# Lower halves and sums of squares of the first mixers on VectorE, and the spatial gate's scale and shift behind its mix

## The chip, the cores and the metric

The kernel runs on one core of a Trainium2 chip. The metric is the device time in microseconds (us) of one execution. The kernel before was timed three times: 3413.01, 3419.14 and 3424.70 us, so the median is 3419.14 us. Its profile is one further execution, with a span of 3426.9 us.

## What is computed

Two transformer blocks run over 512 tokens of 1024 features. Only the first block's mixers are touched by the change, and a part of the second block's memory that is prepared among them:

```
a = rmsnorm(h, g_mix);  z = a @ w_in                       # 1024 -> 2304 features
ya = conformer_conv(z[:768])      # val*sigmoid(gate), 31 taps in time, group layernorm, silu
yb = short_gated_conv(z[768:1536])                         # 3 taps, two gates
yc = spatial_gating(z[1536:])                              # below
h  = h + concatenate([ya, yb, yc]) @ w_out                 # then the experts, block 2, ...

def spatial_gating(zc, ln_g, ln_b, w_s, b_s):
    u, v = split(zc)
    v = group_layernorm(v, ln_g, ln_b, 6 heads of 64)      # (v - m) * rstd * g + b
    ws = w_s masked by chunks of 64 positions              # [head, i, j], i and j in 0..127
    mixed = einsum("hij,bnjhc->bnihc", ws, v) + b_s        # over each block of 128 tokens
    return u * mixed
```

The second block needs `rmsnorm(mem) @ w_mem_kv` for 256 memory rows. It depends on nothing else, so the kernel computes it here.

## The kernel before, in words

All products of this part keep float32 accuracy by a split: a raw tile is rounded to a high half on ScalarE (`hi`, line 163), and the low half `raw - hi` is computed by a second engine (line 164). TensorE then makes three products for each pair (lines 180 to 182): high by high, high by low and low by high. `load_split` (line 165) does this for a chunk of weights. It has three raw tiles (`wir`), two high tiles (`wih`) and two low tiles (`wil`), and `eng` names the engine of the low half.

`front` is the part that the change touches. It runs in this order:

1. The norm of the 512 tokens, split into `xh` and `xl`, eight feature tiles of 128x512.
2. Six products `ftile` of 128 features each (24 matmuls of 512 columns) for the conformer's gate and value, which give `y` (line 326).
3. The value half of the spatial gate, token-major, in four chunks of 128x768 weights, evacuated to `vn` (line 340), then its group norm: 24 statistics (lines 343 and 344), a reciprocal root by Newton's method (`rsqrt`, lines 193 to 198), 24 small subtract-and-multiply operations on VectorE (line 352), and scale and shift on GpSimd (lines 353 and 354).
4. Six products for the short convolution (lines 360 to 373), then the mix of `vn` with `wsT` (line 380) and three products `ftile(12 + hp)`.
5. `memprep`: the memory, eight tiles of 128x256, split into `memh` and `meml`, with sums of squares (`sqa`, lines 130 and 132).
6. The long convolution (`cv`, lines 394 and 397): three times 31 operations of 128x512 on VectorE.
7. The conformer's tail (lines 403 to 424): three chains that go back and forth between TensorE, VectorE and ScalarE.
8. `memkv`: eight chunks for keys (24 matmuls of 256 columns) and eight for values (12 matmuls of 512 columns).
9. `w_out`: eight chunks (24 matmuls of 512 columns). The residual is added at line 435, and its split and its sums of squares go to the experts.

The order in the source is not the order on the engines. A scheduler builds one instruction stream per engine ahead of time, and each engine then works through its stream strictly in order. The long convolution, for example, is spread over a stretch of more than 130 us. All weights come in through one DMA queue on SyncE, in order, and a load of `wir` waits until the low half of the chunk three before has been computed.

Before the change, GpSimd computes the low halves of all 43 weight chunks of `front` (15 of `w_in`, 4 of `w_in_v`, 8 and 8 of the memory's keys and values, 8 of `w_out`), the eight low halves of the memory and the sums of squares of memory and residual.

Of the kernel before, what the change touches and what calls it, by code (L numbers as in the profile page):

```python
# [7 lines left out]
F32 = mybir.dt.float32  # L8
# [5 lines left out]
ALU = mybir.AluOpType  # L14
# [5 lines left out]
DT = 3                     # token tiles of the dense expert product; the last tile gathers  # L20
# [13 lines left out]
def _cols():  # L34
    off = 0
    for name, n in (("g_mix", 8), ("g_ffn", 8), ("g_ple", 8), ("g_final", 8), ("g_mix_2", 8),
                    ("g_mem_q_2", 8), ("g_mem_kv_2", 8), ("g_ffn_2", 8), ("g_sb_out_2", 4),
                    ("g_pool_out_2", 4), ("pool_scale_2", 4), ("conv_a_w", 93), ("conv_a_b", 3),
                    ("ln_a_g", 3), ("ln_a_b", 3), ("conv_b_w", 6)):
        COLS[name] = (off, n)  # L40
        off += n
    return off
# [69 lines left out]
class Stat:  # L112
    """sums of squares of tokens, gathered feature tile by feature tile"""
# [26 lines left out]
    def rstd(self, n, eps, name="r4"):  # L140
        """[128 tokens, tiles]"""
        v = self.pool.tile([128, 8], F32, name="rv", tag="rv", bufs=2)[:, :self.nt]
        self.B.nc.vector.tensor_scalar(v, self.ps[:, :self.nt], 1.0 / n, eps, op0=ALU.mult, op1=ALU.add)
        return self.B.rsqrt(v, self.pool, self.nt, name)


class Body:
# [27 lines left out]
    def mm3(self, ps, ab, n, start=True, stop=True):  # L175
        """ab(k) -> (a_hi, a_lo, b_hi, b_lo)"""
# [11 lines left out]
    def rsqrt(self, v, pool, n, name="rq"):  # L188
        """v [128, n] -> 1/sqrt(v), by Newton's method from the exponent's half"""
# [11 lines left out]
    def spread(self, r, nt=4):  # L201
        """[128 tokens, tiles] -> PSUM [128, tokens], the same on every partition"""
# [10 lines left out]
    def norm_split(self, pool, xs, gname, eps, hi, lo, raw=None):  # L213
        """hi/lo[:, k] <- split(rmsnorm(x))"""
# [10 lines left out]
    def prep(self, pool, x, g, hi, lo, stat=None, last=False, eng=None):  # L225
        """split(x * g) of one feature tile; the token's factor comes in after the product"""
# [53 lines left out]
    def front(self, xst):  # L280
        tc, nc, A = self.tc, self.nc, self.A
        hT = self.hT
        gp = nc.gpsimd
        with tc.tile_pool(name="f1", bufs=1) as p, tc.tile_pool(name="f1w", bufs=2) as w, \
# [8 lines left out]
            def wchunk(c):  # L293
                return self.load_split(w, [128, 8, 128], A["w_in"][c], "wi", eng=gp)
# [12 lines left out]
            lnc = p.tile([128, 768], F32, name="lnc")  # L307
            nc.sync.dma_start(lnc, A["rows"][:, 0:768])
# [6 lines left out]
            # y = val * sigmoid(gate), into a left-padded tile  # L315
# [12 lines left out]
            # the value half of the spatial gate, token-major  # L328
# [4 lines left out]
            for k2 in range(4):  # L333
                wc = self.load_split(w, [128, 2, 384], A["w_in_v"][:, 2 * k2:2 * k2 + 2], "wi", eng=gp)
# [13 lines left out]
            for t in range(4):  # L348
                for h in range(6):
                    i = 6 * t + h  # L350
                    x = vn[:, t, 64 * h:64 * h + 64]
                    nc.vector.tensor_scalar(x, x, mv[:, i, 0:1], sd[:, i:i + 1], op0=ALU.subtract, op1=ALU.mult)
                gp.tensor_mul(vn[:, t], vn[:, t], lnc[:, 0:384])
                gp.tensor_add(vn[:, t], vn[:, t], lnc[:, 384:768])
            # short gated conv
# [18 lines left out]
            # spatial gate  # L374
            for hp in range(3):
                pm = self.bank()
                for n in range(4):
                    for q in range(2):
# [4 lines left out]
                nc.vector.tensor_add(m.rearrange("p (n i) -> p n i", n=4), pm.rearrange("p (n i) -> p n i", n=4),  # L383
                                     bs[:, hp:hp + 1].to_broadcast([128, 4, 128]))
# [4 lines left out]
            # the long convolution fills VectorE where nothing else is ready  # L389
# [10 lines left out]
            # conformer tail  # L400
# [27 lines left out]
            # output projection and residual  # L428
            order = [3, 4, 5, 6, 7, 0, 1, 2]
            st1 = Stat(self, sn)  # L430
            for c in range(8):
                wo = self.load_split(w, [128, 8, 128], A["w_out"][c], "wi", eng=gp)
# [8 lines left out]
    def memprep(self, p, sn):  # L441
        """normed memory, split; its tokens' factors"""
# [3 lines left out]
        st = Stat(self, sn, 256)  # L446
        for k in range(8):
            m = p.tile([128, 256], F32, name="mem", bufs=2)
            nc.sync.dma_start(m, A["memT"][:, k])
            self.prep(sn, m, self.col("g_mem_kv_2", k), mh[:, k], ml[:, k], st, k == 7, eng=nc.gpsimd)  # L450
# [3 lines left out]
    def memkv(self, p, w, mh, ml, r, rb):  # L454
        """keys and values of the memory, to DRAM"""
        nc, A = self.nc, self.A
        for c in range(8):
            wt = self.load_split(w, [128, 8, 128], A["w_mem_k"][c], "wi", eng=nc.gpsimd)
# [5 lines left out]
        for c in range(2):  # L464
            ps = [self.bank(), self.bank()]
            for k2 in range(4):
                wt = self.load_split(w, [128, 2, 512], A["w_mem_v"][c, k2], "wi", eng=nc.gpsimd)
# [10 lines left out]
    def peer(self, xst):  # L478
# [3 lines left out]
        with ExitStack() as st:  # L482
# [56 lines left out]
            with tc.tile_pool(name="pv", bufs=1) as pv:  # L539
# [36 lines left out]
                # back to feature-major, onto the residual  # L576
# [17 lines left out]
    def topk(self, p, h, nh, nl, v16, i16, w16, c16, mid):  # L594
# [27 lines left out]
        # sums that can be among the first 16: rank pairs with (i+1)(j+1) <= 16 lie in  # L622
        # rows i of 2^k-1 .. 2^(k+1)-2, columns j < 16/2^k
# [10 lines left out]
    def decode(self, p, i16, w16, c16, g3):  # L634
        """ranks and gates of the chosen, slots in the order (rank, head)"""
# [8 lines left out]
        # position -> k, then i = 2^k-1 + (r 2^k >> 4), j = (r 2^k & 15) >> k, r = position & 15  # L644
# [22 lines left out]
    def keys(self, p, t, ib, f, g, ix3):  # L667
        """keys of the chosen and gates, [slot, token] (dense tiles); rows of the experts, [token, slot]"""
# [79 lines left out]
    def linear(self, p, wap, n, src, evac, kn=8, k0=0):  # L748
        """feature-major product; evac(i, psum) of each feature tile"""
# [6 lines left out]
    def early(self):  # L756
        """operands of the gated embedding that wait for no token"""
# [27 lines left out]
    def middle(self, upto, outer):  # L785
# [4 lines left out]
        with ExitStack() as est:  # L790
# [6 lines left out]
            # gated per-layer embedding, then the norms on both sides of the block boundary  # L797
# [48 lines left out]
    def mixer2(self, p, q, xa, xb, rbz, rz):  # L846
# [41 lines left out]
        # blocks of 128 keys (i) x 128 queries (j >= i), in the order of j - i  # L888
# [12 lines left out]
        # per head: (0) logits and their log-sigmoids, (1) sums over later keys and weights, (2) output  # L901
# [22 lines left out]
        def parts(r, h):  # L924
            # et and, for j - i > 1, its sums over the key tiles i+1 .. j, in halves for TensorE
# [38 lines left out]
        def means(r, g):  # L964
            # trailing means, less the values, in place
# [146 lines left out]
    def attn_out(self, p, xa, est, gst, upto):  # L1112
        """the last residual of the attention; on it the experts' norm, router and rows"""
# [61 lines left out]
        def order(e):  # L1175
            """weights from the second product of an expert to the first of the next"""
# [10 lines left out]
        # choice of experts: posm [token, tile, expert] the token's place in the expert's list + 1, or 0  # L1187
# [29 lines left out]
        # the token's factor in three parts of bfloat16  # L1217
# [14 lines left out]
    def gates2(self):  # L1232
        """gate of each token and expert, in three parts of bfloat16"""
# [12 lines left out]
    def blocks(self):  # L1246
        """ids (b-1)*32+e of the blocks b with count > 128 b"""
# [22 lines left out]
    def places(self, e, pe=None):  # L1270
        """one-hots of the tokens at each of 128 places of an expert's list"""
# [7 lines left out]
    def tokens(self, e, g):  # L1279
        """of each place: token, its factor, its gate; past the list's end out of bounds, 0, 0"""  # L1280
# [23 lines left out]
    def moe(self):  # L1304
# [3 lines left out]
        with ExitStack() as st:  # L1308
# [8 lines left out]
            class Feed:  # L1317
                """the weights in order of use: loads run ahead by the raw tiles, splits by two"""
# [149 lines left out]
            # blocks past the first 128 tokens of an expert  # L1468
# [29 lines left out]
            # last norm  # L1498
# [43 lines left out]
```

## Time and profile before

| | |
|---|---|
| median of three timed runs | 3419.14 us (3413.01 to 3424.70) |
| span of the profiled execution | 3426.9 us, 44407 instructions |
| TensorE matmul busy | 3164.1 us (92%) |
| VectorE busy | 2697.5 us (79%) |
| ScalarE busy | 1757.4 us (51%) |
| GpSimd busy | 1156.6 us (34%) |

The profile gives the execution's span from its first to its last instruction, and no time around it. The span is 7.8 us above the median of the timed runs, so the profiled execution was on the long side. `front` takes about the first 308 us. PE stands for TensorE, DVE for VectorE, ACT for ScalarE, POOL for GpSimd and SP for SyncE. A row of the timeline gives the start of a merged run of like instructions and their time together; what stands in brackets is the idle time of that engine before them and who ended it.

### The profile page before, as it was taken

Reading aid. Unit: us, or ns where it says so; the run is one execution under the profiler, and the core shown is the slowest. Engines: PE = TensorE matmul, PEld = TensorE weight load, DVE = VectorE, ACT = ScalarE, POOL = GpSimd, SP = SyncE. Lnnn points to the kernel's source line nnn. Section 1 sums busy time; section 2 is a strip of 40 time slices with the busy share of each in tenths; the row PEclk is TensorE's granted clock in tenths of the full one; section 3 lists DMA queues with packets and bytes.
Section 4 is the critical chain, followed back from the end, with each engine's and each line's share of the span. In section 5 each row is a group of like instructions: output and inputs, shape, how many; then the busy total and the mean of one; then the engine's idle time right before and its main releaser. Section 6 shows DMA issues by size and latency. Waiting matters only on the chain. (4 is left out here: it accounts for less than half of the span.)

```text
span 3426.9 us, 44407 instructions
## 1 busy us (share of the span) xinstructions
PE 3164.1 (92%) x15477; PEld 2668.5 (78%) x15477; DVE 2697.5 (79%) x4090; ACT 1757.4 (51%) x2297; POOL 1156.6 (34%) x692
## 2 busy tenths in 40 slices
PE   7679887899999999999999898899999999999996
PEld 6567777799999999998778675677777777777774
DVE  7955978777777777776666763899999999999996
ACT  3123256533333333333445533677777777777774
POOL 4446345444444444441162313122222222222221
PEclk9889988999999999999999999999999999999998
DMA  4132223498888888985411234899999999999994
GB/s 141 56 118 73 81 102 151 157 345 297 301 306 294 305 292 302 306 298 193 146 41 60 75 102 147 293 337 339 345 343 335 335 344 344 341 332 334 346 341 169
DMA packets 280388, 819.69 MB, mean 239 GB/s; under 512 B 29664, under 2 KB 92000, under 8 KB 278368
## 3 DMA queue, kind: packets, MB, share of 16 engines
q1 hardware_dynamic: 223904, 659.48, 54.2%
q0 software_dynamic: 46080, 151.04, 13.5%
q10 hardware_dynamic: 10176, 6.29, 0.6%
q8 instruction: 123, 2.02, 0.2%
q14 instruction: 105, 0.86, 0.1%
HBM read 783.13 MB, written 50.33 MB: 243 GB/s over the span
## 5 line engine op out<-in xcount | busy, mean ns | idle before, releaser
L180 PE MATMUL s<-nh,uh 128*128 128x384 f32 x1024 | 350.6, 342 | 9.2 <-ACT uh L163 9.2
L182 PE MATMUL s<-nh,ul 128*128 128x384 f32 x1024 | 349.8, 342 | 3.6 <-POOL ul L164 2.9
L181 PE MATMUL s<-nl,uh 128*128 128x384 f32 x1024 | 349.4, 341 | 0.0
L163 ACT ACTIVATE vh<-vr 128x1024 fp32r<-128x1024 f32 x128 | 135.9, 1061 | 312.6 <-issue 292.7
L554 POOL DMA_INDIRECT gr<-in_u_r_dram,ix x128 | 192.0, 1500 | 263.0 <-DVE dots L557 226.3
L554 POOL DMA_INDIRECT gr<-in_v_r_dram,ix x128 | 194.8, 1522 | 253.9 <-DVE o L560 218.7
L744 PE MATMUL a<-vh,gh 128*128 128x512 f32 x768 | 236.6, 389 | 0.0
L744 PE MATMUL a<-vh,gll 128*128 128x512 f32 x768 | 236.6, 389 | 0.0
L744 PE MATMUL a<-vl,gh 128*128 128x512 f32 x768 | 236.4, 389 | 0.0
L164 DVE TENSOR_TENSOR ul<-ur,uh 128x1024 fp32r<-128x1024 f32 x117 | 144.4, 1234 | 106.1 <-ACT uh L163 106.1
L164 DVE TENSOR_TENSOR vl<-vr,vh 128x1024 fp32r<-128x1024 f32 x128 | 156.6, 1223 | 68.7 <-ACT vh L163 68.7
L180 PEld LDWEIGHTS s<-nh,uh 128*128 128x128 f32 x1024 | 194.7, 190 | 14.2 <-ACT uh L163 10.0
L163 ACT ACTIVATE gh<-gl 128x384 fp32r<-128x384 f32 x128 | 67.2, 525 | 262.2 <-DVE gl L735 262.2
L182 PEld LDWEIGHTS s<-nh,ul 128*128 128x128 f32 x1024 | 194.5, 190 | 4.7 <-POOL ul L164 3.7
L181 PEld LDWEIGHTS s<-nl,uh 128*128 128x128 f32 x1024 | 194.5, 190 | 4.4
L163 ACT ACTIVATE uh<-ur 128x1024 fp32r<-128x1024 f32 x128 | 135.7, 1060 | 81.1 <-PE s L181 66.9
L744 PEld LDWEIGHTS a<-vl,gh 128*128 128x128 f32 x768 | 144.1, 188 | 30.2
L744 PEld LDWEIGHTS a<-vh,gll 128*128 128x128 f32 x768 | 144.1, 188 | 29.9
L560 DVE SCALAR_TENSOR_TENSOR o<-gr,dots,o 128x1024 f32<-128x1024 f32 x128 | 164.2, 1283 | 3.4 <-DMA gr<-in_v_r_dram,ix 0.6
L726 PE MATMUL b<-ga,gb 128*128 128x128 f32 x768 | 122.1, 322 | 44.9 <-DVE gb L716 33.4
L557 DVE CUSTOM_DVE_ANT_0 scr<-gr,n 128x1024 f32<-128x1024 f32 x128 | 156.4, 1222 | 5.0 <-DMA gr<-in_u_r_dram,ix 2.5
L744 PEld LDWEIGHTS a<-vh,gh 128*128 128x128 f32 x768 | 142.6, 188 | 21.4
(6592 smaller groups left out, 9540.6 us busy)
## 6 DMA issues: line engine op xcount, KB each, us to landing
wr<-in_w_dram SPq DMA_DIRECT2D x768, 512.0 KB, 6.3
ur<-in_u_t_dram SPq DMA_DIRECT2D x128, 512.0 KB, 5.0
vr<-in_v_r_dram SPq DMA_DIRECT2D x128, 512.0 KB, 6.7
gd<-stg SPq DMA_DIRECT2D x12, 2048.0 KB, 6.6
gt<-gd SPq DMA_DIRECT2D x32, 768.0 KB, 9.3
wqr<-in_w_q_dram SPq DMA_DIRECT2D x16, 512.0 KB, 3.6
wir<-in_w_in_dram SPq DMA_DIRECT2D x15, 512.0 KB, 3.6
wlr<-in_w_in_dram SPq DMA_DIRECT2D x12, 512.0 KB, 3.7
```

The lines of the kernel that those rows point to most:

```text
L163: self.nc.scalar.activation(hi, raw, AF.Copy)
L164: (eng or self.nc.vector).tensor_sub(lo, raw, hi.bitcast(F32))
L180: mm(ps, ah, bh, start=(k == 0 and start), stop=False)
L181: mm(ps, ah, bl, start=False, stop=False)
L182: mm(ps, al, bh, start=False, stop=(k == n - 1 and stop))
L554: nc.gpsimd.indirect_dma_start(out=r, out_offset=None, in_=src, in_offset=bass.IndirectOffsetOnAxis(ap=ix3[:, i:i + 1], axis=0))
L557: nc.vector.tensor_tensor_reduce(scr, r, n3, op0=ALU.mult, op1=ALU.add, scale=1.0, scalar=0.0, accum_out=dots[:, i:i + 1])
L560: nc.vector.scalar_tensor_tensor(o3, r, dots[:, i:i + 1], o3, op0=ALU.mult, op1=ALU.add)
L726: nc.tensor.matmul(ps[:, 128 * i:128 * i + 128], bb[:, i], a[:, i], start=True, stop=True)
L744: mm(acc[t][c], a[:, ts], v[:, 512 * c:512 * c + 512], start=(e == 0 and a is gh and v is vh), stop=(e == 127 and a is gl))
```

## The change

The low halves and the sums of squares of `front`, `memprep` and `memkv` move from GpSimd to VectorE: 43 weight chunks, 8 memory tiles, and the two sums of squares. The norm of the spatial gate is applied to all four token tiles at once, by two operations of 128x1536 with broadcast operands, where there were 24. Its scale and shift no longer touch `vn`. Since the mix sums over positions and not over features, `sum_j ws[i,j] * (n[j,c] * g[c] + b[c])` equals `g[c] * (sum_j ws[i,j] * n[j,c]) + b[c] * sum_j ws[i,j]`. So the scale is applied to the result of the mix, and the shift times the row sums of `ws` is added to `bs` beforehand. The row sums are six small matmuls of ones with `wsT`. The columns `ln_c_g` and `ln_c_b` come in with `cols`, and the load of `lnc` (128x768) goes away. The diff's core, without the many comments that it also deletes:

```
-                return self.load_split(w, [128, 8, 128], A["w_in"][c], "wi", eng=gp)
+                return self.load_split(w, [128, 8, 128], A["w_in"][c], "wi")
...
-            lnc = p.tile([128, 768], F32, name="lnc")
-            nc.sync.dma_start(lnc, A["rows"][:, 0:768])
...
-                wc = self.load_split(w, [128, 2, 384], A["w_in_v"][:, 2 * k2:2 * k2 + 2], "wi", eng=gp)
+                wc = self.load_split(w, [128, 2, 384], A["w_in_v"][:, 2 * k2:2 * k2 + 2], "wi")
...
-            for t in range(4):
-                for h in range(6):
-                    i = 6 * t + h
-                    x = vn[:, t, 64 * h:64 * h + 64]
-                    nc.vector.tensor_scalar(x, x, mv[:, i, 0:1], sd[:, i:i + 1], op0=ALU.subtract, op1=ALU.mult)
-                gp.tensor_mul(vn[:, t], vn[:, t], lnc[:, 0:384])
-                gp.tensor_add(vn[:, t], vn[:, t], lnc[:, 384:768])
+            v3 = vn.rearrange("p t (h c) -> p (t h) c", c=64)
+            nc.vector.tensor_tensor(v3, v3, mv[:, :, 0:1].to_broadcast([128, 24, 64]), op=ALU.subtract)
+            nc.vector.tensor_tensor(v3, v3, sd.rearrange("p (i o) -> p i o", o=1).to_broadcast([128, 24, 64]), op=ALU.mult)
...
+            bw = self.bank("x")
+            for h in range(6):
+                nc.tensor.matmul(bw[64 * (h % 2):64 * (h % 2) + 64, 128 * (h // 2):128 * (h // 2) + 128],
+                                 self.ones[:, 0:64], wsT[:, h], start=True, stop=True)
+            for hp in range(3):
+                nc.vector.scalar_tensor_tensor(bs[:, hp], bw[:, 128 * hp:128 * hp + 128], self.col("ln_c_b", hp), bs[:, hp],
+                                               op0=ALU.mult, op1=ALU.add)
...
-                nc.vector.tensor_add(m.rearrange("p (n i) -> p n i", n=4), pm.rearrange("p (n i) -> p n i", n=4),
-                                     bs[:, hp:hp + 1].to_broadcast([128, 4, 128]))
+                nc.vector.scalar_tensor_tensor(m.rearrange("p (n i) -> p n i", n=4), pm.rearrange("p (n i) -> p n i", n=4),
+                                               self.col("ln_c_g", hp), bs[:, hp:hp + 1].to_broadcast([128, 4, 128]),
+                                               op0=ALU.mult, op1=ALU.add)
...
-            st1 = Stat(self, sn)
+            st1 = Stat(self, sn, eng=nc.vector)
...
-                wo = self.load_split(w, [128, 8, 128], A["w_out"][c], "wi", eng=gp)
+                wo = self.load_split(w, [128, 8, 128], A["w_out"][c], "wi")
...
-        st = Stat(self, sn, 256)
+        st = Stat(self, sn, 256, eng=nc.vector)
...
-            self.prep(sn, m, self.col("g_mem_kv_2", k), mh[:, k], ml[:, k], st, k == 7, eng=nc.gpsimd)
+            self.prep(sn, m, self.col("g_mem_kv_2", k), mh[:, k], ml[:, k], st, k == 7)
...
-            wt = self.load_split(w, [128, 8, 128], A["w_mem_k"][c], "wi", eng=nc.gpsimd)
+            wt = self.load_split(w, [128, 8, 128], A["w_mem_k"][c], "wi")
...
-                wt = self.load_split(w, [128, 2, 512], A["w_mem_v"][c, k2], "wi", eng=nc.gpsimd)
+                wt = self.load_split(w, [128, 2, 512], A["w_mem_v"][c, k2], "wi")
```

The scheduler makes new streams for `front`. Behind `front` the streams of all engines are as before. Three places show what moves.

The first is GpSimd's stream at the spatial gate's norm, before. `wil` is a chunk's low half, `vn` the value half of the gate, `lnc` its scale and shift.

```order
L164 TENSOR_TENSOR wil<-wir,wih 128x1024 x4
L353 TENSOR_TENSOR vn<-vn,lnc 128x384
L354 TENSOR_TENSOR vn<-vn,lnc 128x384
L353 TENSOR_TENSOR vn<-vn,lnc 128x384
L354 TENSOR_TENSOR vn<-vn,lnc 128x384
L353 TENSOR_TENSOR vn<-vn,lnc 128x384
L164 TENSOR_TENSOR wil<-wir,wih 128x1024
L354 TENSOR_TENSOR vn<-vn,lnc 128x384
L353 TENSOR_TENSOR vn<-vn,lnc 128x384
L354 TENSOR_TENSOR vn<-vn,lnc 128x384
L164 TENSOR_TENSOR wil<-wir,wih 128x1024 x23
```

Now GpSimd's stream begins with the query weights of the experts (`wql`), behind all of this. The low half that stood among the scale and shift operations, and every other one of `front`, is gone from it.

The second place is VectorE's stream where the memory's first key chunk is split, now. `cv` is the long convolution, `rmem` the memory's reciprocal root.

```order
L398 SCALAR_TENSOR_TENSOR cv<-y,cols,cv 128x512
L194 TENSOR_SCALAR rmem<-rmem 128x2
L398 SCALAR_TENSOR_TENSOR cv<-y,cols,cv 128x512
L196 TENSOR_TENSOR rt<-rmem 128x2
L398 SCALAR_TENSOR_TENSOR cv<-y,cols,cv 128x512
L197 SCALAR_TENSOR_TENSOR rt<-rt,rv 128x2
L398 SCALAR_TENSOR_TENSOR cv<-y,cols,cv 128x512
L198 SCALAR_TENSOR_TENSOR rmem<-rt,rmem 128x2
L164 TENSOR_TENSOR wil<-wir,wih 128x1024
```

The low half of that chunk now stands behind convolution taps that alternate with the root's steps: eleven of them since the split of the gate's second product, five since the last product of `w_in`. Before, it stood on GpSimd, where no convolution is.

The third is the end of the conformer's tail on VectorE, before and then now. `rb` is the root spread for a transpose, `ce` the conformer's tile, `ml` its low half, and line 435 (now 436) adds the first residual.

```order
L418 COPY rb<-rq 128x128 x4
L420 TENSOR_TENSOR ce<-ce,x 128x512
L422 TENSOR_SCALAR ce<-ce,cols 128x512
L423 TENSOR_TENSOR ce<-ce,sq 128x512
L164 TENSOR_TENSOR ml<-ce,mh 128x512
L435 TENSOR_TENSOR hT<-hT,b 128x512
```

```order
L419 COPY rb<-rq 128x128 x4
L421 TENSOR_TENSOR ce<-ce,x 128x512
L164 TENSOR_TENSOR wil<-wir,wih 128x1024
L423 TENSOR_SCALAR ce<-ce,cols 128x512
L424 TENSOR_TENSOR ce<-ce,sq 128x512
L164 TENSOR_TENSOR wil<-wir,wih 128x1024
L164 TENSOR_TENSOR ml<-ce,mh 128x512
L164 TENSOR_TENSOR wil<-wir,wih 128x1024 x3
L436 TENSOR_TENSOR hT<-hT,b 128x512
```

Seven of the eight low halves of the memory's values now stand ahead of the conformer's last low half; the eighth and the first two of `w_out` stand between it and the first residual.

## Rows read from the trace of the kernel before

**Rows 1.** Stretches of the span: busy us by engine, granted clock, DMA share, GB/s.

```profile
20.00:236.00 216.00, 163.60 (x784) 135.63 (x785) 184.72 (x308) 57.96 (x83) 101.61 (x56) 0.88 0.26 80
236.00:252.00 16.00, 14.22 (x60) 10.81 (x59) 0.00 (x0) 6.58 (x8) 11.50 (x5) 1.00 0.66 202
252.00:304.00 52.00, 46.93 (x194) 37.15 (x193) 26.75 (x24) 18.53 (x26) 34.41 (x17) 0.96 0.33 105
```

**Rows 2.** Waits of TensorE, 0 to 310 us: total, times, longest.

```profile
PE b L182 <- POOL wil L164: 31.0, 10, 18.5
```

**Rows 3.** VectorE's timeline: start, us, then the instructions.

```profile
120.59 4.05 DVE L397 SCALAR_TENSOR_TENSOR cv<-y,cols,cv 128x512 f32<-128x512 f32 x6
124.57 1.24 DVE L394 TENSOR_SCALAR cv<-y,cols 128x512 f32<-128x512 f32 x1
...
154.38 6.04 DVE L397 SCALAR_TENSOR_TENSOR cv<-y,cols,cv 128x512 f32<-128x512 f32 x5
160.34 0.68 DVE L386 TENSOR_TENSOR mx<-mx,b 128x512 f32<-128x512 f32 x1
160.94 0.74 DVE L397 SCALAR_TENSOR_TENSOR cv<-y,cols,cv 128x512 f32<-128x512 f32 x1
```

**Rows 4.** GpSimd's timeline, the only work in that time.

```profile
154.35 2.38 POOL L164 TENSOR_TENSOR wil<-wir,wih 128x1024 fp32r<-128x1024 f32 x1 [6.49 <-ACT wih L163]
```

**Rows 5.** VectorE's groups, 20 to 236 us: busy us, mean ns, idle before.

```profile
L397 DVE SCALAR_TENSOR_TENSOR cv<-y,cols,cv 128x512 f32<-128x512 f32 x90 | 93.0, 1065 | 0.5
L352 DVE TENSOR_SCALAR vn<-vn,mv,rq 128x64 f32<-128x64 f32 x24 | 12.0, 581 | 0.0
L164 DVE TENSOR_TENSOR xl<-nt,xh 128x512 fp32r<-128x512 f32 x8 | 9.3, 1172 | 0.0
L198 DVE SCALAR_TENSOR_TENSOR rq<-rt,rq 128x8 f32<-128x8 f32 x9 | 5.7, 637 | 0.2
L196 DVE TENSOR_TENSOR rt<-rq 128x8 f32<-128x8 f32 x9 | 5.7, 630 | 0.3
L369 DVE TENSOR_SCALAR cb<-yb,cols 128x512 f32<-128x512 f32 x2 | 5.3, 2628 | 0.0
...
L229 DVE TENSOR_SCALAR nt<-mem,cols 128x256 f32<-128x256 f32 x8 | 4.1, 514 | 13.4 <-DMA mem<-in_memT_dram 13.4
...
L164 DVE TENSOR_TENSOR ml<-ce,mh 128x512 fp32r<-128x512 f32 x3 | 3.8, 1275 | 1.6 <-ACT mh L163 1.6
...
L197 DVE SCALAR_TENSOR_TENSOR rt<-rt,rv 128x2 f32<-128x2 f32 x3 | 2.6, 868 | 0.0
L193 DVE TENSOR_SCALAR rq<-vv 128x8 int32<-128x8 int32 x3 | 2.4, 803 | 0.1
...
L197 DVE SCALAR_TENSOR_TENSOR rt<-rt,vv 128x8 f32<-128x8 f32 x9 | 1.5, 163 | 0.2
```

**Rows 6.** GpSimd's groups, 20 to 236 us.

```profile
L164 POOL TENSOR_TENSOR wil<-wir,wih 128x1024 fp32r<-128x1024 f32 (+1 forms) x32 | 79.7, 2494 | 108.3 <-ACT wih L163 108.3
```

**Rows 7.** The page's costliest groups: a low half of 128x1024 on VectorE.

```profile
L164 DVE TENSOR_TENSOR vl<-vr,vh 128x1024 fp32r<-128x1024 f32 x128 | 156.6, 1223 | 68.7 <-ACT vh L163 68.7
```

**Rows 8.** ScalarE's timeline: evacuations of the first and fourth chunk of the short convolution.

```profile
84.78 0.58 ACT L360 ACTIVATE bc<-b 128x512 f32<-128x512 f32 x1
...
101.10 0.58 ACT L360 ACTIVATE bc<-b 128x512 f32<-128x512 f32 x1
```

**Rows 9.** TensorE's timeline: two waits for a low half.

```profile
119.27 0.79 PE L182 MATMUL b<-xh,wil 128*128 128x512 f32 x1 [18.54 <-POOL wil L164]
...
271.06 0.50 PE L182 MATMUL b<-mh,wil 128*128 128x512 f32 x1 [2.16 <-POOL wil L164]
```

**Rows 10.** VectorE's timeline: the first residual and the last two.

```profile
257.22 0.69 DVE L435 TENSOR_TENSOR hT<-hT,b 128x512 f32<-128x512 f32 x1 [21.49 <-PE b L182]
...
294.90 0.69 DVE L435 TENSOR_TENSOR hT<-hT,b 128x512 f32<-128x512 f32 x1 [1.60 <-PE b L182]
...
300.53 0.69 DVE L435 TENSOR_TENSOR hT<-hT,b 128x512 f32<-128x512 f32 x1 [2.23 <-PE b L182]
```

More of the change, by code (lines that the diff above doesn't have):

```diff
@@ L38, in _cols @@
                     ("g_pool_out_2", 4), ("pool_scale_2", 4), ("conv_a_w", 93), ("conv_a_b", 3),
-                    ("ln_a_g", 3), ("ln_a_b", 3), ("conv_b_w", 6)):
+                    ("ln_a_g", 3), ("ln_a_b", 3), ("conv_b_w", 6), ("ln_c_g", 3), ("ln_c_b", 3)):
         COLS[name] = (off, n)
@@ L282, in front @@
         hT = self.hT
-        gp = nc.gpsimd
         with tc.tile_pool(name="f1", bufs=1) as p, tc.tile_pool(name="f1w", bufs=2) as w, \
```

## The prediction

> **What bounds the kernel now.** I first read the stretches of the span, to see which engine is full in the part that the change touches. From 20 to 236 us VectorE is busy 184.7 of 216 us, TensorE 163.6 at a mean granted clock of 0.88; from 236 to 252 VectorE does nothing; from 252 to 304 TensorE is busy 46.9 of 52 [rows 1]. The first of these ends with the conformer's last low half, the second is the rest of the memory's values, the third the output projection. Next I read who lets TensorE wait: the low halves made by GpSimd, 31.0 us in 10 waits, one of 18.5 [rows 2]. That one stands at 119.27 [rows 9]: in GpSimd's stream that low half is queued behind scale and shift of `vn`, and these wait for VectorE.
>
> Then I asked whether VectorE's busy time is work. Six taps of the long convolution run from 120.59 to the next start at 124.57, 0.663 us each. Five taps from 154.38 to 160.34 should take 3.3 and take 5.96 [rows 3]. GpSimd's one operation in that time starts at 154.35 and lasts 2.38 [rows 4]: VectorE lost about as much as GpSimd worked. So VectorE's groups are to be read for their excess over an undisturbed instruction. An operation of 128x512 shows 0.68 and occupies 0.60, start to start (160.34 to 160.94, rows 3); the last 0.08 of an instruction lies beside the next.
>
> Excess from 20 to 236 us [rows 5]: convolution 93.0 less 90 x 0.663 = 33.3; `xl` 9.3 less 8 x 0.60 = 4.5; the root's steps, undisturbed 0.163, at lines 198 and 196 5.7 less 9 x 0.163 = 4.2 each, at line 197 2.6 less 0.5 = 2.1, at line 193 2.4 less 0.5 = 1.9; line 369 5.3 less 2 x 0.60 = 4.1; the conformer's `ml` 3.8 less 3 x 0.60 = 2.0. Together 56.3. The groups not shown have more; all of it is at most GpSimd's busy time of 101.6 [rows 1], and I take 5 for them. So 61 of VectorE's 184.7 us are standing still.
>
> **The change part by part, on VectorE from 20 to 236 us.**
>
> *Goes:* the 61 us, since GpSimd has nothing left to do there.
>
> *Norm of the gate:* 24 operations, 12.0 us with their own stalls [rows 5], become two of 128x1536. A 128x1024 operation of two inputs shows 1.223 [rows 7] and so occupies 1.15; 512 columns more add 0.55, so 1.70 each and 3.4 for both. That is 8.6 less. Broadcast operands don't appear in a row; bounds are 2 x 1.15 and, at half speed, 2 x 3.4.
>
> *Comes:* GpSimd's 32 low halves [rows 6], four of them of 768 columns: 28 x 1.15 + 4 x 0.87 (between 0.60 and 1.15) = 35.7. Eight memory low halves and eight steps of their sums of squares, 256 columns, by 0.35 (0.60 less 256 columns at 1 ns): 5.6. Three shifts into `bs`, 0.2 each. Together 41.9.
>
> Sum: -61 - 8.6 + 41.9 = -28 us. GpSimd took 79.7 us for its 32 low halves [rows 6] and VectorE pays 35.7.
>
> *Idle time:* VectorE idles 216 - 184.7 = 31 us there, 13.4 of them for the memory's tiles to arrive [rows 5], the rest mostly in the conformer's chains. The new stream puts low halves and memory work between the former, and the last part of the convolution between the steps of the first chain; I take 10 of the 31 as filled, between -10 (new waits) and 20. VectorE ends this stretch, so it ends 38 us earlier.
>
> *TensorE there:* a `w_in` chunk takes (101.10 - 84.78) / 3 = 5.44 us [rows 8]; 15 of them, four value chunks (96 matmuls of 384 columns, 16.3) and eight key chunks (192 of 256 columns, 21.8) make 120 us: it has room. What is late next: the low half of a chunk now queues behind VectorE's work. at the gate's 48 small statistics operations (0.08 each start to start, by 0.163 less the 0.08 beside the next: some 4 us) I expect a wait of 2 to 3 us, and at the first key chunk, whose low half stands behind eleven taps of 0.663, one of some 8 us. Both lie in VectorE's sum.
>
> *Six row-sum matmuls:* TensorE runs them while it waits for the first split tile: nothing; without this cover under 2 us. The missing load of `lnc`: nothing, the first matmul waits for the norm.
>
> *Values of the memory:* 16 us from 236 to 252 [rows 1] with VectorE empty. In the new stream seven of eight low halves are done before the conformer ends. One to two chunks of 2.7 us (12 matmuls at 5.44 / 24) are left, so 6 us: -10, between 0 and -13.
>
> *Output projection:* seven steps from 257.22 to 300.53 take 43.3 us; an undisturbed one takes 5.63 [rows 10], seven 39.4. The 3.9 of excess hang on one low half that came late at 271.06 [rows 9], behind two low halves of query weights on GpSimd. These stay and can still stop VectorE for their 5 us, but it has more than 2 us of slack in each step: -3, between +2 and -4. The last sum of squares is shorter on VectorE: under 1 us, left out.
>
> Sum: -38 - 10 - 3 = -51 us. Behind this part every stream is unchanged and starts with the residual's norm, so the rest moves forward as a whole. The profiled execution (span 3426.9) would come to 3376; it is 7.8 above the median of the timed runs, and from that median 3419.1 - 51 = 3368 us.
>
> The Trainium skill speaks against the change as well as for it (Perfetto Trace Analysis, section Optimizing Scalar/DVE Operations): if VectorE is saturated, moving work off it, even to GpSimd, may make sense; but the two share a read port, so moving work between them might not help. By the first half the kernel gets slower, as in the second rival; by the second, the forecast holds. The row of five taps above bears out the second half.
>
> **Rivals.**
>
> *Waits in place of stalls (0.15).* VectorE's stream is now one line in which a low half stands behind taps, and a tap behind a wait for TensorE. Only the excess that rows show counts, 56.3 + 8.6 - 41.9 = 23 us, and nothing is gained on idle time, values or projection: 3419 - 23 = 3396 us. For it: TensorE's clock falls in such waits (mean 0.88 now), so that each is paid twice. Against it: the waits now last up to 18.5 us already.
>
> *Slower (0.04).* The long spells of VectorE's operations are not GpSimd's doing, and stay. Then a full engine gets 41.9 us more and loses 8.6: 3419 + 33 = 3452 us. It decides wherever a tap takes over 1 us with GpSimd empty. Against it: begin and length of the excess in the two timelines.
>
> *More (0.10).* The hidden stalls are 10 us more, and 16 us rather than 10 of idle time are filled: 3419 - 67 = 3352 us.
>
> *Not on the path (0.03).* The experts' start waits for something else, such as query weights: 3419 us. Against it: the first residual waits 21.49 us for TensorE [rows 10], and all that follows needs the last one.
>
> **How the numbers follow.** The forecast has 0.68. What a measurement of this kernel can tell from no change is about 0.3%, 10 us. Forecast, first and third rival lie below that: 0.93 faster; 0.03 the same; 0.04 slower. The range from 3348 to 3398 takes in the first and third rival and the bounds of idle time; what lies outside it is the second and fourth, and part of the mishaps that add up.
>
> **What will show it.** Right: no tap longer than 0.75 us until the query weights; the conformer's last low half near 198 us (the stretch that it ends reached to 236); the first residual near 209, the last near 249; the clock of the first 200 us above 0.9; no wait of 18 us for a low half, but some of 2 to 9. Wrong: taps over 1 us with GpSimd empty; a low half of 128x1024 that occupies more than 1.3 us; residuals more than 6 us apart; or a first residual near 209 with a later stage that is longer by the same amount.

## The result and the profile after

The changed kernel takes 3355.99 us, the median of four runs (3354.76 to 3360.70), beside 3419.66 us for the kernel before in the same call: a ratio of 0.982, with a 95% interval from 0.9806 to 0.9835. That is 63.7 us less. The forecast was 3368 us with a range from 3348 to 3398, so the time lies in the range, 12 us below the likeliest value. The profiled execution of the kernel after has a span of 3354.4 us; that of the kernel before was on the long side (3426.9 us), so the two spans differ by 72.5 us and the medians by 63.7. What is read from a trace is one execution's.

The first rows are stretches of the span of the kernel after; the columns are those of [rows 1], and 193.1 us is the end of the conformer's last low half, which ended at 235.7 in the kernel before.

```profile
20.00:193.10 173.10, 163.91 (x820) 136.12 (x819) 160.61 (x338) 60.43 (x86) 0.00 (x0) 0.95 0.36 111
193.10:204.10 11.00, 11.00 (x48) 8.82 (x47) 3.70 (x4) 4.50 (x6) 0.00 (x0) 1.00 0.75 231
204.10:249.10 45.00, 42.52 (x186) 34.04 (x185) 30.00 (x51) 16.90 (x24) 5.75 (x2) 1.00 0.27 90
```

GpSimd's column is empty up to 193 us. VectorE is busy 160.6 us where it was busy 184.7, although it now makes every low half, and it idles 12.5 us where it idled 31.0 (215.7 less 184.7). TensorE gets through 820 matmuls in 173 us, where it got through 784 in 216, at a clock of 0.95 instead of 0.88.

VectorE's timeline shows where the time went. The six taps at 94.58 take 4.05 us, as the undisturbed six of [rows 3] did, and the work that came from GpSimd stands among them; five taps that take 6.04 us are not to be found any more: the longest of the 90 taps takes 0.754 us.

```profile
91.11 1.75 DVE L347 TENSOR_TENSOR vn<-vn,rq 128x1536 f32<-128x1536 f32 x1
92.78 0.74 DVE L398 SCALAR_TENSOR_TENSOR cv<-y,cols,cv 128x512 f32<-128x512 f32 x1
93.44 1.21 DVE L164 TENSOR_TENSOR wil<-wir,wih 128x1024 fp32r<-128x1024 f32 x1
94.58 4.05 DVE L398 SCALAR_TENSOR_TENSOR cv<-y,cols,cv 128x512 f32<-128x512 f32 x6
98.74 1.22 DVE L164 TENSOR_TENSOR wil<-wir,wih 128x1024 fp32r<-128x1024 f32 x1
```

VectorE's groups from 20 to 193 us answer to [rows 5] (busy us, then the mean ns of one). The taps fell from 1065 to 743 ns, the low halves `xl` from 1172 to 683, the root's steps from 637 to 162.

```profile
L398 DVE SCALAR_TENSOR_TENSOR cv<-y,cols,cv 128x512 f32<-128x512 f32 x90 | 64.4, 743 | 0.2
L164 DVE TENSOR_TENSOR wil<-wir,wih 128x1024 fp32r<-128x1024 f32 x30 | 36.5, 1218 | 1.4 <-ACT wih L163 1.2
L164 DVE TENSOR_TENSOR xl<-nt,xh 128x512 fp32r<-128x512 f32 x8 | 5.1, 683 | 0.0
L164 DVE TENSOR_TENSOR wil<-wir,wih 128x768 fp32r<-128x768 f32 x4 | 3.8, 952 | 0.0
...
L198 DVE SCALAR_TENSOR_TENSOR rq<-rt,rq 128x8 f32<-128x8 f32 x9 | 1.5, 162 | 0.2
```

TensorE's waits for a low half up to 310 us (total, times, longest) were 31.0 us in ten [rows 2]; now VectorE is the one that it waits for, 6.0 us in three.

```profile
PE b L182 <- DVE wil L164: 6.0, 3, 4.9
```

The end of the part, on VectorE: the conformer's last low half, the first residual and the last, and the end of the root of the residual's norm. The residuals were at 257.22 and 300.53 [rows 10].

```profile
192.40 0.68 DVE L164 TENSOR_TENSOR ml<-ce,mh 128x512 fp32r<-128x512 f32 x1
...
204.07 0.69 DVE L436 TENSOR_TENSOR hT<-hT,b 128x512 f32<-128x512 f32 x1 [2.73 <-PE b L182]
...
243.42 0.69 DVE L436 TENSOR_TENSOR hT<-hT,b 128x512 f32<-128x512 f32 x1 [2.88 <-PE b L182]
...
249.08 0.17 DVE L439 COPY r<-r 128x4 f32<-128x4 f32 x1
```

The first residual comes 53.2 us earlier and the last 57.1. Behind them nothing is given back.

### The profile page after: what moved, and what is told of

Same layout as the page of the kernel before. It is cut to its first block, busy times and chain, and to the rows that moved or that the text cites. A ratio compares the mean times of both kernels' runs of the same rounds, so it can differ in the third digit from the quotient of the medians.

```text
span 3354.4 us, 44364 instructions
## 1 busy us (share of the span) xinstructions
PE 3139.9 (94%) x15489; PEld 2645.6 (79%) x15489; DVE 2679.3 (80%) x4138; ACT 1756.8 (52%) x2297; POOL 1014.4 (30%) x617
## 5 line engine op out<-in xcount | busy, mean ns | idle before, releaser
L164 DVE TENSOR_TENSOR vl<-vr,vh 128x1024 fp32r<-128x1024 f32 x128 | 156.6, 1224 | 67.7 <-ACT vh L163 67.7
L180 PEld LDWEIGHTS s<-nh,uh 128*128 128x128 f32 x1024 | 195.7, 191 | 14.7 <-ACT uh L163 10.5
L727 PE MATMUL b<-ga,gb 128*128 128x128 f32 x768 | 118.8, 315 | 44.2 <-DVE gb L717 34.8
```

The source lines that it names most:

```text
L164: (eng or self.nc.vector).tensor_sub(lo, raw, hi.bitcast(F32))
L180: mm(ps, ah, bh, start=(k == 0 and start), stop=False)
L727: nc.tensor.matmul(ps[:, 128 * i:128 * i + 128], bb[:, i], a[:, i], start=True, stop=True)
```

## The experiments

The theory: VectorE's operations with two inputs stand still while GpSimd's read data, for as long as GpSimd's operation lasts; the change pays because it takes such pairs away. Its rivals: the long spells of VectorE have another cause; what paid is the shorter way of a low half through the queues, or the cheaper norm; or any work on GpSimd at all disturbs, reading or not. Ten kernels were run.

### GpSimd works beside an unchanged stream

`pool_reads` is the kernel after with 35 subtractions on GpSimd, one behind each of the chunks of weights up to the memory's values, whose results nobody uses. All other engines have the streams of the kernel after. (A tap is an operation at line 398 in the kernel after; added lines move it to 409 and 408 in the next two kernels.)

```
+    def idle(self, hi):
+        f = hi.rearrange("p a b -> p (a b)").bitcast(F32)
+        n = min(896, f.shape[-1])
+        self.nc.gpsimd.tensor_sub(self.dm[:, :n], f[:, :n], self.call[:, :n])
```

> The changed kernel, with one more operation on GpSimd for each of the 35 weight chunks ahead of the output projection: it subtracts a constant tile from the chunk's high half (128x896, or 128x768) into a tile that nobody reads. The result is unchanged, and the streams of all other engines are those of the changed kernel, instruction for instruction. Theory (GpSimd's reading operations stop VectorE): 35 operations of about 2.1 us are some 75 us; VectorE has work during most of them, so taps of the long convolution take up to 2.9 us again, VectorE's stretch grows by 40 to 60 us and the time goes to 3395 to 3415 us. Rival (only the latency and the queue of GpSimd's low halves cost time, a busy GpSimd costs nothing): within 5 us of the changed kernel, 3356 us, and taps stay at 0.74 us.

Measured: 3411.7 us (3405.61 to 3415.53), 0.9971 of before, interval 0.996 to 0.9982. Nothing but idle GpSimd was put to work, and 55.7 of the 63.7 us are gone again. They go in this part: the residual's norm ends at 303.50 us, 54.4 later than in the kernel after. In the groups from 20 to 250 us of this kernel the taps are back at 964 ns, the low halves at 1394 instead of 1224; the last row is from VectorE's timeline:

```profile
L409 DVE SCALAR_TENSOR_TENSOR cv<-y,cols,cv 128x512 f32<-128x512 f32 x90 | 84.5, 964 | 0.2
L164 DVE TENSOR_TENSOR wil<-wir,wih 128x1024 fp32r<-128x1024 f32 x32 | 44.5, 1394 | 1.8 <-ACT wih L163 1.8
...
303.50 0.17 DVE L450 COPY r<-r 128x4 f32<-128x4 f32 x1
```

```profile
L178 POOL TENSOR_TENSOR dm<-wih,consts 128x896 f32<-128x896 f32 x30 | 73.1, 2437 | 132.5 <-ACT wih L163 132.4
```

The subtractions read `wih`, so ScalarE could also have had to wait for them before it fills that tile again. It did so once, for 2.1 us.

`pool_writes` has 105 fills of the same tile instead, which read nothing. They wait for nothing either, so they run back to back from 0.74 us on for 95.9 us, where the subtractions are spread over the whole part.

```
+    def idle(self, hi):
+        for _ in range(3):
+            self.nc.gpsimd.memset(self.dm, 0.0)
```

> The changed kernel, with 105 memsets of 128x896 on GpSimd into a tile that nobody reads, from the start of the program on: GpSimd is busy for some 80 to 100 us, but reads nothing. All other streams are those of the changed kernel. Theory (only GpSimd operations that read stop VectorE's operations of two inputs): within 5 us of 3356 us, and taps of the long convolution at 0.74 us while GpSimd runs. Rival (any GpSimd access stops VectorE): 40 us or more on top, as with the reading operations. By the first theory's own limit, one-input operations of 128x512 may still be stopped a few times: up to 5 us.

Measured: 3357.15 us (3355.60 to 3359.91), 0.9812 (0.9793 to 0.9832): the time of the kernel after. The fills end at 96.7 us, so only the groups from 20 to 97 us can tell. The 36 taps in that time take 747 ns each, the longest 0.805 us. In `pool_reads` 26 taps lie in the same stretch, beside 29.5 us of subtractions; they take 991 ns, the longest 2.614 us. So a GpSimd that only writes does not stop the taps, and its busy share alone says nothing of the disturbance. One kind of operation did suffer: the `nt` of the memory, a `tensor_scalar` with one tensor input, took 734 ns where it takes 347 in the kernel after; for eight of them that is 3.1 us.

```profile
L408 DVE SCALAR_TENSOR_TENSOR cv<-y,cols,cv 128x512 f32<-128x512 f32 x36 | 25.6, 747 | 0.1
...
L233 DVE TENSOR_SCALAR nt<-mem,cols 128x256 f32<-128x256 f32 x8 | 5.8, 734 | 2.1 <-DMA mem<-in_memT_dram 2.1
```

```profile
0.74 95.92 POOL L177 MEMSET dm<- 128x896 f32 x105 [0.29 <-POOLq L1544]
```

The row of the taps in `pool_reads`, from 20 to 97 us:

```profile
L409 DVE SCALAR_TENSOR_TENSOR cv<-y,cols,cv 128x512 f32<-128x512 f32 x26 | 24.6, 991 | 0.1
```

The Trainium skill (SBUF — State Buffer, section Who interferes with whom) states it so: a VectorE instruction with two inputs in SBUF contends with a GpSimd instruction that reads SBUF, and not with one that only writes; a `tensor_scalar`, in a mode that takes both port pairs, can contend with GpSimd too. The first half agrees with the taps, 991 against 747 ns. The second agrees with the `nt`, 734 against 347 ns, if they run in such a mode, which no row here shows.

### The parts of the change apart

`norm_only` keeps the new norm and puts every low half and sum of squares of this part back on GpSimd; `halves_only` is the reverse, the old norm with its scale and shift on GpSimd; `vn_on_dve` is the kernel before with nothing but that scale and shift on VectorE.

```
# norm_only, against the kernel after, and so at each load_split and Stat of the part
-                return self.load_split(w, [128, 8, 128], A["w_in"][c], "wi")
+                return self.load_split(w, [128, 8, 128], A["w_in"][c], "wi", eng=nc.gpsimd)
# vn_on_dve, against the kernel before
-                gp.tensor_mul(vn[:, t], vn[:, t], lnc[:, 0:384])
-                gp.tensor_add(vn[:, t], vn[:, t], lnc[:, 384:768])
+                nc.vector.tensor_mul(vn[:, t], vn[:, t], lnc[:, 0:384])
+                nc.vector.tensor_add(vn[:, t], vn[:, t], lnc[:, 384:768])
```

> Only the second half of the change: the gate's norm in two operations and its scale and shift behind the mix, with every low half and sum of squares still on GpSimd. Theory (the stalls are the main cost): the 24 small operations give back 8.6 us, scale and shift no longer stop VectorE (another 5 to 10 us), and TensorE's wait of 18.5 us mostly goes, but VectorE is still stopped by 32 low halves: 3395 to 3405 us. Rival (the queue at the gate's norm was the main cost): most of the whole gain, 3370 to 3380 us.

Measured: 3407.31 us (3401.96 to 3412.74), 0.9952 (0.9936 to 0.9968), just outside of what was expected: against 3420.22 us for the kernel before in those calls the norm alone is worth 12.9 us. The wait of 18.5 us is gone, but TensorE still waits 10.2 us in five for GpSimd's low halves, and the taps stay at 976 ns:

```profile
L398 DVE SCALAR_TENSOR_TENSOR cv<-y,cols,cv 128x512 f32<-128x512 f32 x90 | 85.0, 976 | 0.5
```

> Only the first half of the change: all low halves and sums of squares of the front on VectorE, the gate's norm with its 24 operations and GpSimd's scale and shift as before. Theory (the stalls are the main cost): 40 to 50 of the 64 us, so 3370 to 3380 us; the 24 operations and eight GpSimd operations still cost some 15 to 20 us of VectorE. Rival (the queue at the norm): under half of the gain, 3390 us or more, since TensorE's wait there stays.

Measured: 3373.45 us (3369.07 to 3378.05), 0.9863 (0.9843 to 0.9883), as expected. The halves alone bring 46.8 us against the same 3420.22 us, and here the taps fall to 759 ns. 46.8 and 12.9 make 59.7 of the 63.7, so the parts nearly add up.

```profile
L397 DVE SCALAR_TENSOR_TENSOR cv<-y,cols,cv 128x512 f32<-128x512 f32 x90 | 66.1, 759 | 0.2
```

> The kernel before, with only the gate's scale and shift (four multiplications and four additions of 128x384) moved from GpSimd to VectorE; nothing else. It takes the low half out from behind them on GpSimd. Theory (stalls): VectorE pays 8 x 0.45 = 3.6 us and is spared up to 11.8 us of GpSimd's work: 5 to 10 us less than before, about 3412 us. Rival (the queue at the norm): TensorE's wait of 18.5 us goes and brings 15 us or more: 3405 us or less.

Measured: 3412.37 us (3407.47 to 3414.99), 0.9979 (0.9969 to 0.9989). The low half that stood behind scale and shift on GpSimd no longer does: TensorE's waits for GpSimd's low halves fall from 31.0 us to 10.3, the longest from 18.5 to 2.7, although a wait of 11.3 us for scale and shift themselves comes in. All this is worth 6.5 us of the 63.7 (3418.87 for the kernel before in these calls). That the queue at the norm was the main thing is refuted.

### The same move in other places

`out_back` is the kernel after with the low halves of `w_out` and the residual's sums of squares back on GpSimd; `stat_dve` has the sums of squares that are left on GpSimd, behind this part, on VectorE as well.

```
# out_back
-            st1 = Stat(self, sn, eng=nc.vector)
+            st1 = Stat(self, sn)
-                wo = self.load_split(w, [128, 8, 128], A["w_out"][c], "wi")
+                wo = self.load_split(w, [128, 8, 128], A["w_out"][c], "wi", eng=nc.gpsimd)
# stat_dve
-        self.eng = eng or B.nc.gpsimd
+        self.eng = eng or B.nc.vector
```

> The changed kernel with only the output projection's eight low halves and its sums of squares back on GpSimd. By the prediction's term for this part: the late low half and the longer last sum of squares come back, 4 to 6 us more than the changed kernel, so 3360 to 3362 us, with one of seven residual steps of 9 us and six of 5.6. Rival (VectorE has slack there, so nothing is at stake): 3356 us, all steps 5.6 us.

Measured: 3361.11 us (3359.05 to 3361.95), 0.983 (0.9815 to 0.9846), 5.1 above the kernel after, as expected. The two intervals overlap, but the trace shows it too: the residual's norm ends at 253.48 instead of 249.08 us. So something is at stake here, though little; the late step between two residuals is one of 7.4 us, not 9.

> The changed kernel, with all other sums of squares (middle of the kernel and second block) on VectorE too. They are some 60 GpSimd operations of 128x512, 1.3 to 1.5 us each, in stretches where TensorE is busy over 90%. Theory: VectorE gains a little and pays 0.60 for each, TensorE sets the pace there: within 5 us of the changed kernel, 3351 to 3361 us. Rival (stalls cost time everywhere): 10 us less or better.

Measured: 3361.76 us (3358.43 to 3363.26), 0.9834 (0.9818 to 0.985), just above the range and no gain. Why it gains nothing was not followed up.

`wq_dve` is the kernel after with the low halves of the query weights (`wql`) and of the normed residual (`nl`) on VectorE, which leaves GpSimd without work from 20 to 360 us.

```
-                    self.split(nraw[:, k], nh[:, k], nl[:, k], nc.gpsimd)
+                    self.split(nraw[:, k], nh[:, k], nl[:, k])
-            wq = self.load_split(self.wqp, [128, 8, 128], A["w_q"][2 * h + j], "wq", rb=2, eng=nc.gpsimd)
+            wq = self.load_split(self.wqp, [128, 8, 128], A["w_q"][2 * h + j], "wq", rb=2)
```

> The changed kernel, with the 16 low halves of the experts' query weights and the eight of the normed tokens also on VectorE; GpSimd does 48 us of work for them now. If a busy GpSimd costs VectorE time wherever it reads, this brings 10 us or more. By the theory it does not: VectorE's long operations there have one input (MAX8, FIND_INDEX8, MATCH_REPLACE8) and are not stopped, so VectorE only gets 16 x 1.15 + 8 x 0.60 = 23 us more; TensorE sets the pace with 5.44 us a chunk: between 3 us less and 8 us more than the changed kernel, 3353 to 3364 us.

Measured: 3387.48 us (3379.99 to 3393.37), 0.9908 (0.9891 to 0.9925). This is a plain miss: 31 us slower than the kernel after. The groups from 250 to 450 us of VectorE say why, first of the kernel after, then of this one. In the first, GpSimd works on `wql` and `nl` for 43 us in that time, beside VectorE's search for the largest sixteen:

```profile
L600 DVE FIND_INDEX8 i<-v,b 128x8 uint32<-128x128 f32 x64 | 18.4, 288 | 0.0
L599 DVE MAX8 v<-b 128x8 f32<-128x128 f32 x64 | 18.4, 287 | 1.8 <-PE b L619 1.8
```

```profile
L600 DVE FIND_INDEX8 i<-v,b 128x8 uint32<-128x128 f32 x64 | 18.5, 289 | 0.0
L599 DVE MAX8 v<-b 128x8 f32<-128x128 f32 x64 | 18.4, 288 | 1.4 <-PE b L619 1.4
...
L164 DVE TENSOR_TENSOR wql<-wqr,wqh 128x1024 fp32r<-128x1024 f32 x14 | 17.0, 1216 | 8.1 <-ACT wqh L163 8.0
```

Each of these instructions runs over one tile of data, and takes the same 288 ns with GpSimd at work and without (the forms with `mr` between 275 and 283 in both; `b` lies in PSUM, `mr` in SBUF): there was no stall to win back. What came was 17.0 us for `wql` and 5.1 for `nl`, on an engine that had little room. In the stretch from 300 to 360 us of the kernel after VectorE is busy 59.4 of 60 us:

```profile
300.00:360.00 60.00, 57.77 (x290) 48.49 (x288) 59.41 (x435) 12.01 (x17) 18.71 (x8) 1.00 0.20 60
```

```profile
300.00:360.00 60.00, 51.81 (x242) 42.54 (x241) 56.80 (x358) 10.79 (x14) 0.00 (x0) 0.94 0.26 79
```

In `wq_dve`, whose row is the second, TensorE's granted clock is 0.94 where it had been 1.00, and its waits from 240 to 460 us have a new entry:

```profile
PE b L182 <- DVE wql L164: 13.5, 3, 4.9
```

So VectorE's work is on the path there, and the first product of the gates' gather moves from 419.6 to 448.4 us. Between the end of the residual's norm and that product VectorE is busy 172.7 of 198.9 us, where it was busy 145.6 of 170.3. Of the 28.6 us, 27.1 are thus longer work and 1.5 idle time:

```profile
249.30:419.60 170.30, 150.12 (x757) 130.33 (x755) 145.60 (x847) 56.79 (x74) 67.91 (x32) 0.94 0.26 81
```

```profile
249.50:448.40 198.90, 159.43 (x762) 135.47 (x760) 172.66 (x868) 51.50 (x70) 24.92 (x10) 0.89 0.22 71
```

The low halves are 22.1 of the work. Another 4.0 are the `cand`, small two-input operations; in `wq_dve` three of them fall beside GpSimd's next low halves (`ul`) and take 4.50 us. The rows are VectorE's and GpSimd's timeline:

```profile
394.55 0.21 DVE L631 TENSOR_TENSOR cand<-v 128x64 f32<-128x64 f32 x1
...
394.95 4.50 DVE L631 TENSOR_TENSOR cand<-v 128x64 f32<-128x64 f32 x3
```

```profile
394.59 4.71 POOL L164 TENSOR_TENSOR ul<-ur,uh 128x1024 fp32r<-128x1024 f32 x2 [394.14 <-DMA ur<-in_u_t_dram]
```

The gates' gather, from 419 to 607 us, is the opposite case: there VectorE works on two-input operations and TensorE waits for it 34.8 us. `ga_dve` is the kernel after with GpSimd's products `ga` of that stage on VectorE; `ga_mix` gives also twelve more of them to ScalarE.

```
# ga_dve and ga_mix
-                nc.gpsimd.tensor_mul(a, e.rearrange("p k t -> p t k"),
+                nc.vector.tensor_mul(a, e.rearrange("p k t -> p t k"),
# ga_mix alone: which of each eight go to ScalarE
-GACT = (0, 3, 6)
+GACT = (0, 2, 4, 6)
```

> The kernel after with the products ga of the gather of the gates (60 of the 96, 128x512 from bfloat16, 1.69 us each on GpSimd) on VectorE too, so that GpSimd does no arithmetic on data from 419 to 634 us. Here VectorE works on two-input operations, unlike the query stage: in the kernel after gb takes 1.005 us each against 0.68 where GpSimd is idle (95 of them, 30.9 us over), eq 1.096 against 0.68 (47, 19.6 us over), and the one-hot products some 6 us over. Theory (a two-input operation of VectorE waits for GpSimd's): these 57 us go and 60 operations of some 0.68 us, 41 us, come; VectorE's queue is 16 us shorter, and since TensorE waits 34.8 us there for gb, the time falls by 5 to 16 us: 3340 to 3351 us. Rival (as with the query weights, where 23 us more on VectorE made the kernel 31 us longer): what counts is the number of operations in VectorE's queue, and the time rises by 10 to 41 us: 3366 to 3397 us.

Measured: 3337.40 us (3333.35 to 3340.12), 0.9754 (0.9738 to 0.9769): 18.6 us below the kernel after, whose interval (0.9806 to 0.9835) lies wholly above, and 3 below the best expected. The groups of VectorE from 410 to 634 us, of the kernel after and of `ga_dve`:

```profile
L717 DVE TENSOR_TENSOR gb<-consts,tr 128x512 f32<-128x512 f32 x96 | 94.3, 1002 | 19.2 <-PE b L727 18.4
L710 DVE TENSOR_TENSOR eq<-iota,trb 128x1024 bf16<-128x1024 bf16 x48 | 51.7, 1087 | 1.2 <-POOL ga L724 1.2
```

```profile
L717 DVE TENSOR_TENSOR gb<-consts,tr 128x512 f32<-128x512 f32 x96 | 65.8, 687 | 2.9 <-PE b L727 2.0
L724 DVE TENSOR_TENSOR ga<-eq,tr 128x512 f32<-128x512 bf16 x60 | 64.0, 1072 | 0.0
L710 DVE TENSOR_TENSOR eq<-iota,trb 128x1024 bf16<-128x1024 bf16 x48 | 36.4, 777 | 0.0
```

An operation of `gb` fell from 1002 to 687 ns. A `ga` costs 1.07 us on VectorE and not the 0.68 that was assumed, so the 64.0 us that came are more than the 43.8 that `gb` and `eq` gave back. VectorE's queue did not get shorter, as the expectation had it. But VectorE had idled 19.2 us before `gb`, waiting for TensorE, and that fell to 2.9. TensorE's waits for `gb` fell from 34.8 to 3.1 us; 10.9 us of waits for `ga` on VectorE came in (the rows below, of the kernel after and of `ga_dve`), and those for ScalarE stayed at 8.4. The last gate product starts at 587.5 instead of 607.1 us. In the kernel after, GpSimd's `ga` had themselves waited 57.0 us for TensorE. What paid, the shorter `gb` and `eq` or the way of a `ga` without GpSimd, was not separated.

```profile
PE b L727 <- DVE gb L717: 34.8, 33, 2.2
```

```profile
PE b L727 <- DVE ga L724: 10.9, 11, 2.2
...
PE b L727 <- DVE gb L717: 3.1, 8, 0.6
```

> As ga_dve, with half of the products ga on ScalarE in place of three in eight (twelve more of them, four activations of 0.52 us each, on an engine that is busy 134 of 215 us there) and half on VectorE. Theory: VectorE's queue loses another 12 x 0.68 = 8 us, and ScalarE gains 25 us, still 159 of 215 us: 3334 to 3349 us, below ga_dve if VectorE sets the pace, above it if TensorE then waits for ScalarE's products (8.4 us of waits for them in the kernel after). Rival: as for ga_dve, 3360 to 3390 us.

Measured: 3329.57 us (3323.97 to 3333.43), 0.973 (0.9713 to 0.9747), again below the range, by 4. The gather's last product starts at 576.6. This is the fastest kernel of the study, 26 us below the kernel after and 90.7 below its own runs of the kernel before. TensorE's waits for operands of these products, from 410 to 634 us, are down to 13.0 us, from 43.9 in the kernel after; these rows hold 11.0 of them:

```profile
PE b L727 <- ACT ga L722: 6.6, 13, 2.4
PE b L727 <- DVE gb L717: 4.4, 8, 2.1
```

## Why the prediction was right, point by point

**The mechanism** was right. That VectorE loses what GpSimd works was read from one pair of rows [rows 3, 4]; `pool_reads` shows it, since it adds nothing but GpSimd's work to the streams of the kernel after and gives back 55.7 us. `pool_writes` adds that work which only writes does not do this, for the stretch up to 97 us. The second rival (long spells that stay) is refuted: with GpSimd empty, no tap took over 0.754 us.

**VectorE from 20 to 236 us.** Forecast 38 us earlier, measured 42.6 (235.7 to 193.1). Both terms were mis-sized, in opposite ways. Busy time was to fall by 28 and fell by 24.1 (184.7 to 160.6): the taps lost 28.6 us, not 33.3. The prediction had compared a group's busy time, in which the tail of each instruction counts unless its neighbour is a tap too, with an interval from start to start, which leaves the tail out. The count of low halves was short too: 34 stand in this stretch of the kernel after (30 and 4 in the groups above), where the sum took GpSimd's 32, although the prediction's own term for the values has seven of their eight done ahead; by its 1.15 each the two that are missing are 2.3 us. Idle time was to fall by 10, at most 20, and fell by 18.5 (31.0 to 12.5). This is the term that was most off, and that the two errors partly cancel is luck. The norm went as forecast: its two operations of 128x1536 take 1.75 us each, 1.67 from start to start (91.11 to 92.78), beside the 1.70 assumed, so the broadcast operands cost nothing.

**The waits** were forecast at two places. At the first key chunk TensorE waited 4.9 us, not 8; at the gate's statistics it did not wait for a low half at all, because the half that it needed next was finished before them. The first rival (waits in place of stalls) falls with this: 31.0 us became 6.0.

**Values of the memory.** From the conformer's last low half to the first residual there are now 11.0 us, fully busy on TensorE, after 21.5 (235.7 to 257.2): -10.5, forecast -10.

**Output projection.** Seven steps take 39.35 us (243.42 less 204.07) after 43.31 [rows 10]: -4.0, forecast -3, and the 39.4 of undisturbed steps was right to 0.1. GpSimd's two `wql` do fall into it, from 211.79 us on for 5.75. VectorE waits 3.0 us for a high half that ScalarE rounds behind those of the query weights, and then a low half and an `xl` beside `wql` take 1.42 and 2.88 us instead of 1.22 and 0.68. The third residual comes 8.92 us behind the second (209.70 to 218.62). That is more than the 6 us that the prediction had named as a sign of being wrong, and it came about beside the two `wql` that the prediction had allowed for. But TensorE never waited for a low half there, and the later steps catch up.

**What was left out.** The residual's norm ends 58.6 us earlier (249.08, before 307.68), 1.5 more than the last residual, which is the last sum of squares. The first operation behind it, VectorE's `nraw`, gains another 2.1. It waits for two chunks of query products. In the kernel before, TensorE's granted clock was 0.66 from 302 to 312 us, and the first of these products took 0.63 us each; in the kernel after it was 1.00 from 244 to 254, and they took 0.39. By the medians about 3 us more come behind that, and no single place was shown for them.

The gain of 63.7 us is 12.7 more than the forecast's 51. Of these, 4.6 are the first stretch, 0.5 the values, 1.0 the projection, and 6.6 what was left out. The third rival (more, 3352 us) named the right direction: its filled idle time came, its hidden stalls did not.

## What to carry to other kernels

An operation's time is read against the undisturbed one of the same shape; where a two-input VectorE operation is longer and GpSimd reads data at the same moment, moving GpSimd's work onto VectorE can free both, even if VectorE looks full. Before the move, look at what VectorE does beside it: with two-input work the move paid 47 us (taps, by the low halves alone) and 19 us (`gb`, cause not separated), with the searches it cost 31. What the moved operation costs on VectorE matters less than whether the engine that sets the pace waits for it.

## What was not expected of the hardware

GpSimd busy 96 us with pure fills left the 36 taps beside them at 747 ns and the kernel's time unchanged, and yet doubled a one-input `tensor_scalar` (347 to 734 ns). The searches (`MAX8`, `FIND_INDEX8`) did not feel GpSimd's subtractions at all: 287 and 288 ns with them, 288 and 289 without, and those that read `mr` 275 and 283 ns with them, 276 and 283 without. And a multiplication of 128x512 with a transposed bfloat16 operand took 1.07 us on VectorE, where two float32 operands take 0.69.
